# The last feed-forward layer: one more inner block without the seven-product scheme, and products 5 and 2 exchanged in a group's last unit

## The chip, the cores and the metric

The kernel runs on one core of one Trainium2 chip. The time is the device time of one execution in microseconds (us). The kernel before was timed three times: 1418.72 us in the median, 1417.37 to 1418.97 us. Its profile is of a further execution, which took 1418.3 us, and whose span from the first to the last instruction is 1416.1 us.

The engines carry these names in the profile: PE (matrix multiply), PEld (its weight loads), DVE (vector engine), ACT (scalar engine), POOL, and SP, which issues the transfers from memory.

## The reference

Two layers of a transformer-like network act on 128 context tokens and 512 latent tokens of width 1024. Layer 0 has a pooling and convolution mixer, layer 1 has attention; each is followed by a SwiGLU feed-forward network (FFN) with inner width 2816. Everything is in 32-bit floating point. The change lies in the FFN of layer 1, which is the last large piece of work:

```python
D_FF = ((8 * D_MODEL // 3 + 255) // 256) * 256      # 2816

def swiglu(h, w_in, w_out):
    a, b = jnp.split(h @ w_in, 2, axis=-1)
    return (jax.nn.silu(a) * b) @ w_out

        h = modulate(x, norm_g[l, 1], sh2, sc2)
        x = x + g2 * swiglu(h, w_ffn_in[l], w_ffn_out[l])
    y_sample = rms_norm(x, final_g)
```

`modulate` is an RMS norm with a scale and a shift, one pair for the context tokens and one for the latent tokens. The final RMS norm is all that follows this FFN.

## The kernel before

**Layout.** Activations are held transposed: the features lie on the 128 partitions, in eight blocks `k`, and all 640 tokens lie along the free dimension, in two halves of 320. Both token groups go through together. Each 32-bit operand is split into a high and a low part (`wh`, `wl` for weights, `ah`/`al`, `bh`/`bl`, `xh`/`xl` for activations); a matrix product is the sum of three matmuls: high by high, high by low, low by high. The split of a tile is always the same pair of instructions, the high part by ACT (L142) and then the low part by DVE (L143).

**The FFN in groups.** The 22 inner blocks of 128 go in three groups, 0 to 7, 8 to 15 and 16 to 21. A group first computes its inner blocks (`fi`, input projection, SiLU and product; in names `fi1_0_5` is layer 1, group 0, projection 5), keeps them as `ah`/`al` (`keep`), and then adds its part of the output projection to `x` (`fo`).

**Plain blocks.** In layer 1 the inner blocks 0 to `PLAIN - 1` are computed plainly: two projections for each block (the `a` half, then the `b` half), each of eight `k` by three matmuls by two token halves, 48 matmuls of 128x320. They work on the scaled but not yet normalised `x` and multiply by `rstd` afterwards (L503), so they can start before the norm is there. Their results are evacuated by DVE and ACT (`ea`, `eb`).

**Seven products.** All other inner blocks of layer 1 (`fast_blocks`) are units of seven products, in place of the eight block products of a 2x2 by 2x2 multiplication: the 1024 input features are halved, the tokens are halved, and the block's `a` and `b` halves are the two column blocks. A product is four `k` by three matmuls of 128x320, so a unit is 84 matmuls where a plain block is 96. In exchange DVE has to form sums of weights (`weight`, L228 to L239, on the raw weights in place) and, once, sums of the normalised activations (`operand_in`, which calls `Ops.make`): for each of four `kk`, two normalised tiles `n`, a tile `tt` of differences, and seven operands of 320 tokens, split into `bh`/`bl` and `xh`/`xl`. This operand work is put behind the plain projections 1 to 4 (`in_done`), amid their own evacuations.

The products accumulate in three PSUM banks: products 1 and 2 in `x1` (bank 0), products 6, 5 and 3 in `y` (bank 1), products 7 and 4 in `w` (bank 2); odd and even units use different halves of each bank. After product 1, ACT copies `x1` to `y` (L620), so 6 must wait for that copy. After 6, ACT copies `y` out (L623), so the next product on `y` must wait for it. After 2, ACT takes the SiLU of `x1` (L626). After 5, ACT copies `y` out (L629) and DVE adds `w` to it (L630), so 3 must wait for the copy. After 3, ACT takes the SiLU of `y` (L632). After 4, DVE adds `w` and multiplies by the SiLU (L635, L636), and the block is kept. `fast_order` gives the order of the products: while unit n does 1, 7, 6, 2, 5, the products 3 and 4 of unit n - 1 are put between them. Behind the last unit there is nothing more to put between its products 5, 3 and 4.

**What sets the order.** Outside the start of the kernel the instructions of each engine are put in order by the scheduler of the tile framework when the program is built; each engine then works through its own queue strictly in that order. Split weights live in tiles of two products each with three buffers (`wh`, `wl`), named by the first of the two (`wh_fi1_3_p1` holds products 1 and 7 of block 3). Raw weights have three buffers, 1 MB each, loaded by SP (L218). PSUM tiles of the plain projections and of `fo` take the three banks in turn (`ps_tile`), so the number of projections ahead decides which bank comes next.

## Time and profile before

| what | value |
| --- | --- |
| median of 3 runs | 1418.72 us (1417.37 to 1418.97) |
| profiled execution | 1418.3 us, of it 1416.1 us span |
| busy in the span | PE 1363.3 us (96%), DVE 1011.2 us (71%), ACT 580.2 us (41%), POOL 148.4 us (10%) |
| granted PE clock, mean of the span | 0.980 |
| FFN of layer 1, first matmul of `fi` | 947.5 us |
| first matmul of a seven-product unit | 992.6 us |
| last matmul of a seven-product unit | 1358.3 us |

PE is busy almost throughout, so what the program costs is the number of matmuls, the time that each takes, and the few places where PE stands still or runs at a lower clock. A row of the timeline gives start, duration, engine, line, operation, tiles and, in brackets, how long the engine stood idle before it and which instruction ended that. A row of the windows gives, for a stretch, busy time and number of instructions of each engine (an instruction that reaches over an edge counts in both stretches), then the granted PE clock (1.00 is full speed), the busy share of the transfer engines and GB/s. Matmuls overlap: one of 0.31 us is followed by the next 0.147 to 0.149 us later.

### The profile page before, as it was taken

How to read it: one execution, taken by the hardware profiler on the slowest of the kernel's cores; microseconds unless marked ns; L12 is line 12 of the kernel's file. 1: busy time of each engine (PE TensorE's matmuls, PEld its weight loads, DVE VectorE, ACT ScalarE, POOL GpSimd, SP SyncE). 2: the span in 40 equal slices, each digit the busy share in tenths (PEclk: the TensorE clock that was granted, in tenths of full speed). 3: DMA queues.
4: the chain of work that ended last, by engine and by line, in shares of the span. 5: the costliest groups of instructions: out<-in, count | busy, mean ns of one | idle time of the engine just before them, and what ended most of it. 6: DMA issues, size and time to landing. Idle time of an engine off the chain costs nothing.

```text
span 1416.1 us, 22537 instructions
## 1 busy us (share of the span) xinstructions
PE 1363.3 (96%) x9127; PEld 1332.6 (94%) x9127; DVE 1011.2 (71%) x1963; ACT 580.2 (41%) x1031; POOL 148.4 (10%) x116
## 2 busy tenths in 40 slices
PE   6989998999999999999999999999899999999995
PEld 3889998999999999999999999999899999999995
DVE  4899999777768787754667677688863477536745
ACT  3433334332123221222565676557552255314543
POOL 3451112000000000000303121030000000000003
PEclk7999999999999999999999999999899999999998
DMA  9624544444444444221322111011132022311212
GB/s 364 253 95 161 189 141 161 138 151 147 146 152 145 154 137 161 79 86 59 113 73 92 46 46 38 31 60 60 38 112 90 31 90 89 120 60 60 75 46 75
DMA packets 36728, 154.50 MB, mean 109 GB/s; under 512 B 3984, under 2 KB 11152, under 8 KB 26000
## 3 DMA queue, kind: packets, MB, share of 16 engines
q1 hardware_dynamic: 36624, 153.07, 31.0%
q8 instruction: 71, 1.16, 0.3%
q14 instruction: 33, 0.27, 0.1%
HBM read 147.55 MB, written 2.88 MB: 106 GB/s over the span
## 4 chain that ended last, share of the span: by engine, by line
PE 75%; DVE 18%; issue 2%; ACT 2%; DMA 1%; POOL 1%; SPq 0%; DVEq 0%; POOLq 0%; ACTq 0%
PE fi L285 22%; PE fo L285 21%; PE fi L608 17%; DVE junk L363 6%; PE pq L285 5%; PE wa L285 2%; DVE al L467 2%; PE o L1287 2%; PE s L1237 1%; DVE bl L143 1%; DVE wl_in L143 1%; PE t L1270 1%; DVE x L488 1%; DVE wl_out L143 1%; DMA raw_ada<-wada 1%
## 5 line engine op out<-in xcount | busy, mean ns | idle before, releaser
L363 DVE CUSTOM_DVE_ANT_0 junk<-rawa,silb 128x512 f32<-128x512 f32 x336 | 250.6, 746 | 7.6 <-ACT silb L791 1.0
L285 PE MATMUL fi<-al,wh_fi 128*128 128x320 f32 (+1 forms) x800 | 184.6, 312 | 2.2 <-DVE al L467 2.2
L285 PE MATMUL fi<-ah,wh_fi 128*128 128x320 f32 (+1 forms) x800 | 185.0, 313 | 1.4 <-ACT ah L465 1.4
L285 PE MATMUL fi<-ah,wl_fi 128*128 128x320 f32 (+1 forms) x800 | 184.3, 312 | 0.0
L488 DVE SCALAR_TENSOR_TENSOR x<-fo,mod,x 128x128 f32<-128x128 f32 (+1 forms) x144 | 54.6, 434 | 135.0 <-PE fo L285 131.7
L285 PEld LDWEIGHTS fi<-al,wh_fi 128*128 128x128 f32 x800 | 136.0, 190 | 2.7 <-DVE al L467 2.7
L285 PEld LDWEIGHTS fi<-ah,wh_fi 128*128 128x128 f32 x800 | 136.3, 191 | 1.6 <-ACT ah L465 1.6
L285 PEld LDWEIGHTS fi<-ah,wl_fi 128*128 128x128 f32 x800 | 135.8, 190 | 0.0
L143 DVE TENSOR_TENSOR wl_fi_p<-raw_fi,wh_fi_p 128x512 fp32r<-128x512 f32 x133 | 90.1, 688 | 53.9 <-ACT wh_fi_p L142 53.9
L142 ACT ACTIVATE wh_fi_p<-raw_fi 128x512 fp32r<-128x512 f32 x133 | 81.0, 627 | 110.8 <-PE fi L608 66.0
L142 ACT ACTIVATE wh_fi<-raw_fi 128x1024 fp32r<-128x1024 f32 x50 | 52.9, 1059 | 171.8 <-PE fi L285 134.6
L142 ACT ACTIVATE wh_fo<-raw_fo 128x1024 fp32r<-128x1024 f32 (+1 forms) x48 | 47.5, 990 | 178.9 <-PE fo L285 131.2
L608 PE MATMUL fi<-bh,wh_fi_p 128*128 128x320 f32 x304 | 94.7, 311 | 4.1 <-ACT bh L142 2.2
L608 PE MATMUL fi<-bl,wh_fi_p 128*128 128x320 f32 x304 | 94.2, 310 | 0.5 <-DVE bl L143 0.5
L608 PE MATMUL fi<-bh,wl_fi_p 128*128 128x320 f32 x304 | 94.5, 311 | 0.0
L285 PE MATMUL fo<-bh,wh_fo 128*128 128x320 f32 x352 | 80.6, 310 | 0.0
L285 PE MATMUL fo<-bh,wl_fo 128*128 128x320 f32 x352 | 80.5, 310 | 0.0
L285 PE MATMUL fo<-bl,wh_fo 128*128 128x320 f32 x352 | 80.4, 310 | 0.0
L422 POOL TENSOR_TENSOR ssq_b<-ssq_b,sq_b 128x640 f32<-128x640 f32 x14 | 25.2, 1803 | 516.1 <-ACT sq_b L420 516.1
L285 PE MATMUL fo<-al,wh_fo 128*128 128x320 f32 x328 | 75.0, 310 | 0.0
L285 PE MATMUL fo<-ah,wl_fo 128*128 128x320 f32 x328 | 74.9, 309 | 0.0
L285 PE MATMUL fo<-ah,wh_fo 128*128 128x320 f32 x328 | 74.8, 309 | 0.0
(342 smaller groups left out, 3348.5 us busy)
## 6 DMA issues: line engine op xcount, KB each, us to landing
raw_fi<-wfi SPq DMA_DIRECT2D x44, 1024.0 KB, 4.8
rawa<-wada SPq DMA_DIRECT2D x84, 512.0 KB, 3.5
raw_fo<-wfo SPq DMA_DIRECT2D x16, 1024.0 KB, 4.9
raw_ada<-wada SPq DMA_DIRECT2D x12, 512.0 KB, 9.3
raw_in<-win SPq DMA_DIRECT2D x6, 1024.0 KB, 6.5
raw_fo<-wfo SPq DMA_DIRECT2D x8, 768.0 KB, 4.2
raw_qkv<-wqkv SPq DMA_DIRECT2D x6, 1024.0 KB, 4.8
raw_out<-wout SPq DMA_DIRECT2D x4, 1024.0 KB, 4.9
```

The lines of the kernel that those rows point to most:

```text
L142: S.activation(h, src, AF.Copy)
L143: eng.tensor_tensor(out=l, in0=src, in1=h.bitcast(F32), op=ALU.subtract)
L285: PE.matmul(ps[:, h, 0 : hi - lo], w[a][:, k, cols], rhs[b][:, k0 + k, lo:hi], start=k == 0 and a == b, stop=k == kn - 1 and a == 1,)
L363: op = V.tensor_tensor_reduce(out=junk, in0=raw[:, cols], in1=silb[:, c, cols], scale=1.0, scalar=0.0, op0=ALU.mult, op1=ALU.add, accum_ou ...
L422: (eng or G).tensor_tensor(out=self.acc[:, cols], in0=self.acc[:, cols], in1=sq[:, cols], op=ALU.add)
L467: V.scalar_tensor_tensor(out=lo[:, k, a:b], in0=x[:, k, a:b], scalar=s[:, k, c : c + 1], in1=h[:, k, a:b].bitcast(F32), op0=ALU.mult, op1= ...
L488: V.scalar_tensor_tensor(out=xs, in0=got[:, 0 : b - a], scalar=mod[l][:, gate0 + m, c : c + 1], in1=xs, op0=ALU.mult, op1=ALU.add,)
L608: PE.matmul(out, w[a][:, k, :], ops.get(OPERAND[p], b)[:, k, :], start=fresh and k == 0 and a == b, stop=k == ops.kn - 1 and a == 1, skip_ ...
L1237: PE.matmul(self.ps[:, hf, 0:HT], bufB[a][:, self.h, q0 : q0 + P], kt[b][:, self.kv, hf * HT : hf * HT + HT], start=n == 0, stop=n == 2,)
L1270: PE.transpose(flat(pt)[:, s * P : s * P + P], self.pe[:, s * P : s * P + P], ident)
L1287: PE.matmul(po[:, 0 : 2 * P], vt[a][:, self.kv, s * P : s * P + P], got[b][:, s, :], start=s == 0 and n == 0, stop=s == 4 and n == 2,)
```

## The change

`PLAIN` goes from 3 to 4. Group 0 of the last FFN then computes the blocks 0 to 3 plainly, with eight projections where there were six, and the blocks 4 to 7 in seven products, four units where there were five. Layer 0, which has no seven-product units, stays as it is. The operand work stays behind the projections 1 to 4.

In `fast_order` the last unit of each group (there are three) gets product 5 ahead of product 2. With n the last unit, the order at its end was 1, 7, 3 of n - 1, 6, 4 of n - 1, 2, 5, then 3, 4; it becomes 1, 7, 3 of n - 1, 6, 4 of n - 1, 5, 2, then 3, 4.

```diff
@@ -31,7 +31,7 @@
 GROUPS = ((0, 8), (8, 16), (16, 22))
 
 FAST = (1,)
-PLAIN = 3
+PLAIN = 4
 RAW = 3
 WINDOWS = (2, 4, 8, 16)
 PAD = 8
@@ -178,6 +178,8 @@
         out = []
         for n in range(units + 1):
             seq = ((n, 1), (n, 7), (n - 1, 3), (n, 6), (n - 1, 4), (n, 2), (n, 5))
+            if n == units - 1:
+                seq = seq[:5] + ((n, 5), (n, 2))
             out += [(u, p) for u, p in seq if 0 <= u < units]
         return out
 
```

How this moves the instructions in the built program is shown at three places. Line numbers of the changed kernel are two higher from L181 on; the numbers at the ends of names are buffer numbers.

DVE in group 0, where the operands for `kk` = 3 are formed (`n_7`, `n_3`, `tt`; low parts `bl`, `xl`). Before:

```order
L677 TENSOR_TENSOR n_7_9635<-x_67,rstd_83 128x640
L143 TENSOR_TENSOR wl_fi1_3_p1_9575<-raw_fi1_3_9249,wh_fi1_3_p1_9574 128x512
L143 TENSOR_TENSOR wl_fi1_3_p6_9658<-raw_fi1_3_9249,wh_fi1_3_p6_9657 128x512
L234 TENSOR_TENSOR raw_fi1_3_9249<-raw_fi1_3_9249 128x4x128
L584 TENSOR_TENSOR tt_9639<-n_7_9635,n_3_9631 128x320
L143 TENSOR_TENSOR bl_71<-n_7_9635,bh_70 128x2x320
L585 TENSOR_TENSOR n_3_9631<-n_3_9631 128x320
L143 TENSOR_TENSOR wl_fi1_3_p6_9658<-raw_fi1_3_9249,wh_fi1_3_p6_9657 128x512
L586 TENSOR_TENSOR tt_9639<-n_7_9635,n_3_9631 128x320
L143 TENSOR_TENSOR bl_71<-n_3_9631,bh_70 128x2x320
L589 TENSOR_TENSOR n_7_9635<-n_7_9635,tt_9639 128x320
L143 TENSOR_TENSOR xl_9243<-tt_9639,xh_9242 128x2x320
```

With the change:

```order
L679 TENSOR_TENSOR n_7_9631<-x_67,rstd_83 128x640
L143 TENSOR_TENSOR wl_fi1_3_1_9708<-raw_fi1_3_9249,wh_fi1_3_1_9707 128x1024
L143 TENSOR_TENSOR wl_fi1_4_p1_9714<-raw_fi1_4_9412,wh_fi1_4_p1_9713 128x512
L586 TENSOR_TENSOR tt_9635<-n_7_9631,n_3_9627 128x320
L143 TENSOR_TENSOR bl_71<-n_7_9631,bh_70 128x2x320
L587 TENSOR_TENSOR n_3_9627<-n_3_9627 128x320
L505 TENSOR_TENSOR eb1_2_9701<-fi1_0_5_9648,rstd_83 128x640
L588 TENSOR_TENSOR tt_9635<-n_7_9631,n_3_9627 128x320
L143 TENSOR_TENSOR bl_71<-n_3_9627,bh_70 128x2x320
L591 TENSOR_TENSOR n_7_9631<-n_7_9631,tt_9635 128x320
L143 TENSOR_TENSOR xl_9243<-tt_9635,xh_9242 128x2x320
L143 TENSOR_TENSOR xl_9243<-n_7_9631,xh_9242 128x320
```

The operand rows keep their order. Where four weight rows for products of block 3 stood among them, there are now the second half of block 3's plain weights, the first product of block 4, and the evacuation of projection 5.

PE in group 0, from product 1 to product 6 of the first unit (bank 0 is `fi1_0_0`, bank 1 `fi1_0_1`, bank 2 `fi1_0_2`). Before, the last three matmuls of products 1 and 7, the start of `y` (L602) and then product 6:

```order
L608 MATMUL fi1_0_0_9714<-bh_70,wh_fi1_3_p1_9574 128x320
L608 MATMUL fi1_0_0_9714<-bl_71,wh_fi1_3_p1_9574 128x320
L608 MATMUL fi1_0_0_9714<-bh_70,wl_fi1_3_p1_9575 128x320
L608 MATMUL fi1_0_2_9716<-xh_9242,wh_fi1_3_p1_9574 128x320
L608 MATMUL fi1_0_2_9716<-xl_9243,wh_fi1_3_p1_9574 128x320
L608 MATMUL fi1_0_2_9716<-xh_9242,wl_fi1_3_p1_9575 128x320
L602 MATMUL fi1_0_1_9715<-bh_70,onesr_75 128x320 x2
L608 MATMUL fi1_0_1_9715<-xh_9242,wh_fi1_3_p6_9657 128x320
L608 MATMUL fi1_0_1_9715<-xl_9243,wh_fi1_3_p6_9657 128x320
L608 MATMUL fi1_0_1_9715<-xh_9242,wl_fi1_3_p6_9658 128x320
```

With the change, the same place in block 4:

```order
L610 MATMUL fi1_0_0_9832<-bh_70,wh_fi1_4_p1_9713 128x320
L610 MATMUL fi1_0_0_9832<-bl_71,wh_fi1_4_p1_9713 128x320
L610 MATMUL fi1_0_0_9832<-bh_70,wl_fi1_4_p1_9714 128x320
L610 MATMUL fi1_0_2_9834<-xl_9243,wh_fi1_4_p1_9713 128x320
L610 MATMUL fi1_0_2_9834<-xh_9242,wl_fi1_4_p1_9714 128x320
L610 MATMUL fi1_0_1_9833<-xh_9242,wh_fi1_4_p6_9775 128x320
L610 MATMUL fi1_0_1_9833<-xl_9243,wh_fi1_4_p6_9775 128x320
L610 MATMUL fi1_0_1_9833<-xh_9242,wl_fi1_4_p6_9776 128x320
```

The start of `y` and ten matmuls of product 7 now stand ahead of product 1, and two matmuls of product 7 behind it.

ACT at the end of group 1, from the copy after product 6 of block 15 (`uv` is L623 and L629, `sa` is L626 and L632 before). Before:

```order
L142 ACTIVATE wh_fi1_15_p3_11705<-raw_fi1_15_11410 128x512
L623 ACTIVATE uv_11690<-fi1_1_1_10798 128x320
L142 ACTIVATE wh_fo1_1_0_0_11770<-raw_fo1_1_0_11534 128x1024
L142 ACTIVATE ah_68<-uv_11568 128x640
L626 ACTIVATE sa_11729<-fi1_1_0_10797 128x320
L142 ACTIVATE wh_fo1_1_0_1_11779<-raw_fo1_1_0_11534 128x1024
L629 ACTIVATE uv_11690<-fi1_1_1_10798 128x320
L632 ACTIVATE sa_11729<-fi1_1_1_10798 128x320
```

With the change:

```order
L142 ACTIVATE wh_fi1_15_p3_11701<-raw_fi1_15_11406 128x512
L625 ACTIVATE uv_11686<-fi1_1_1_10794 128x320
L142 ACTIVATE wh_fo1_1_0_0_11766<-raw_fo1_1_0_11530 128x1024
L142 ACTIVATE ah_68<-uv_11564 128x640
L631 ACTIVATE uv_11686<-fi1_1_1_10794 128x320
L142 ACTIVATE wh_fo1_1_0_1_11775<-raw_fo1_1_0_11530 128x1024
L628 ACTIVATE sa_11739<-fi1_1_0_10793 128x320
L634 ACTIVATE sa_11739<-fi1_1_1_10794 128x320
```

The copy after product 5 (L629 before, L631 now) has moved ahead of the split of the second half of `fo`'s first weights.

## The prediction

> **What bounds the kernel now.** I began with the first two parts of the page, to see which engine fills the span.

> ```profile
> span 1416.1 us, 22537 instructions
> ...
> PE 1363.3 (96%) x9127; PEld 1332.6 (94%) x9127; DVE 1011.2 (71%) x1963; ACT 580.2 (41%) x1031; POOL 148.4 (10%) x116
> ...
> PEclk7999999999999999999999999999899999999998
> ```

> PE is busy for 96% of the span. In the row of its clock, each digit stands for a fortieth of the span (35.4 us); the 29th, from 991 to 1027 us, is an 8 amid nines. The changed code runs there. So I asked next for PE's waits from 880 us to the end:

> ```profile
> PE ms_fin L446 <- DVE ssq_fin L422: 2.2, 1, 2.2
> PE fi L608 <- ACT bh L142: 2.2, 1, 2.2
> PE fi L608 <- ACT uv L629: 1.9, 2, 1.4
> PE fi L285 <- DVE al L467: 1.4, 1, 1.4
> ...
> PE fi L608 <- ACT fi L620: 0.6, 1, 0.6
> PE fi L608 <- DVE bl L143: 0.5, 1, 0.5
> PE fi L602 <- ACT eb L508: 0.4, 1, 0.4
> ```

> The columns are total, times, longest. Two places matter. The rows on `bh`, `bl`, `fi` L620 and `eb` are one stretch, where the seven products begin: 3.7 us together. The row on `uv` L629 is the copy after product 5, late at two group ends: 1.9 us. The waits on `ssq_fin` and `al` lie outside the change.

> The waits understate the first place. PE's timeline and the windows:

> ```profile
> 992.61 0.31 PE L608 MATMUL fi<-bh,wh_fi_p 128*128 128x320 f32 x1
> ...
> 995.10 0.31 PE L608 MATMUL fi<-xh,wl_fi_p 128*128 128x320 f32 x1
> 997.61 0.41 PE L608 MATMUL fi<-bh,wh_fi_p 128*128 128x320 f32 x1 [2.20 <-ACT bh L142]
> 998.51 0.63 PE L608 MATMUL fi<-bl,wh_fi_p 128*128 128x320 f32 x1 [0.48 <-DVE bl L143]
> ```

> ```profile
> 956.79:992.53 35.74, 35.74 (x243) 35.74 (x242) 31.42 (x52) 27.12 (x52) 0.00 (x0) 1.00 0.17 60
> 965.02:999.99 34.97, 32.28 (x210) 31.42 (x209) 33.93 (x58) 27.53 (x50) 0.00 (x0) 0.97 0.09 31
> 992.60:1008.50 15.90, 12.21 (x51) 10.54 (x50) 14.26 (x25) 7.58 (x14) 0.00 (x0) 0.68 0.00 1
> 1146.00:1171.30 25.30, 25.28 (x169) 24.56 (x169) 19.14 (x31) 13.29 (x27) 0.00 (x0) 1.00 0.25 84
> 994.80:998.20 3.40, 1.02 (x6) 0.53 (x4) 3.40 (x7) 3.21 (x6) 0.00 (x0) 1.00 0.00 0
> 998.20:1008.40 10.20, 8.88 (x29) 7.71 (x30) 8.66 (x15) 2.53 (x6) 0.00 (x0) 0.50 0.00 1
> ```

> From 992.60 to 1008.50 PE started about 50 matmuls. At the rate of two undisturbed units (168 matmuls in 25.30 us, 0.151 us each) these take 7.5 us; they took 15.9. This place loses 8.4 us, less than half of it by standing still. The rest is the clock: from 998.20 to 1008.40 it was granted at 0.50, after 3.4 us in which PE was busy for only 1.02.

> Why are the operands late? DVE was busy for 33.93 of the 34.97 us from 965.02 to 999.99 (its number is the third of the windows). It is the engine behind; the chain of waits says the same:

> ```profile
> 993.37 1.20 DVE wl_fi_p L143 x2
> 994.57 0.60 DVE raw_fi L234
> ...
> 998.85 1.14 DVE xl L143 x2
> 999.99 0.74 DVE eb L503
> ...
> 1000.76 0.18 ACT eb L508
> ```

> DVE forms the last operand (`xl`) at 999.99, when PE has been short of operands since 995.2, and weight conversions for products stand amid the operands.

> **The change part by part.** *Block 3 plain.* The plain stretch from 956.79 to 992.53 holds 240 matmuls in 35.74 us, so 96 take 14.3 us. A unit takes 12.65 us (half of 25.30). So +1.6 us, on PE and so on the path.

> *The start of the seven products.* They now begin 14.3 us later, about 1006.9. I walk DVE's queue from where it first differs, with its timeline:

> ```profile
> 975.25 1.21 DVE L143 TENSOR_TENSOR wl_fi<-raw_fi,wh_fi 128x1024 fp32r<-128x1024 f32 x1
> ...
> 984.81 0.68 DVE L143 TENSOR_TENSOR wl_fi_p<-raw_fi,wh_fi_p 128x512 fp32r<-128x512 f32 x1
> 985.53 0.69 DVE L232 TENSOR_TENSOR raw_fi<-raw_fi 128x512 f32<-128x512 f32 x1
> 986.25 0.69 DVE L236 TENSOR_TENSOR raw_fi<-raw_fi 128x512 f32<-128x512 f32 x1
> 986.86 0.48 DVE L584 TENSOR_TENSOR tt<-n,n 128x320 f32<-128x320 f32 x1
> ```

> Three rows (984.81 to 986.86, 2.05 us) give way to one half of plain weights (1.2 us): 0.85 us sooner. Amid `kk` = 3, four weight rows of 0.6 (2.4) give way to 1.2 for the second half, 0.6 for the first product of block 4, and 0.74 for evacuating projection 5, which stood behind the operands (2.5). So the last operand comes near 999.2, 7.7 us before PE wants it. Up to product 7's weights DVE then has seven instructions (the rest of block 2, the evacuation of projection 6, a weight sum, two splits, one `keep`), at the mean of the stretch (33.93 / 58 = 0.585) 4.1 us: they are there at 1003.3, 3.6 us ahead. The plain block's own weights are split by about 986 and 993.8, and PE wants them at 992.6 and 999.7. DVE's surplus of work is absorbed by block 3, and with the wait goes the clock's reason. This removes 8.4 us.

> Something new appears. Bank 0 is now projection 7's, the last one; product 1 waits for its evacuation (DVE 0.74, ACT 0.18). Ahead of it stand L602 and ten matmuls of product 7, 12 steps of 0.147 (1125.31 to 1125.45 and on, below) or 1.8 us, which cover that. But between product 1 and product 6 only two matmuls of 7 are left to cover the copy L620. Group 1 shows that hand-over with four:

> ```profile
> 1125.31 0.31 PE L608 MATMUL fi<-bh,wl_fi_p 128*128 128x320 f32 x1
> 1125.45 0.31 PE L608 MATMUL fi<-xh,wl_fi_p 128*128 128x320 f32 x1
> ...
> 1125.88 0.31 PE L608 MATMUL fi<-xh,wl_fi_p 128*128 128x320 f32 x1
> 1126.13 0.42 PE L608 MATMUL fi<-xh,wh_fi_p 128*128 128x320 f32 x1
> ```

> From product 1's last matmul (1125.31) to product 6's first (1126.13) are 0.82 us; with two between, PE would need 0.44, so it waits 0.4 us. ACT's queue has a `keep` ahead of that copy, so I take +0.5, with 0 (all covered) and 1.5 (evacuation, 0.9, and a hand-over of 0.6 bare) as bounds.

> *Product 5 ahead of 2.* At the end of group 1 ACT did this, and PE below it:

> ```profile
> 1219.86 1.06 ACT L142 ACTIVATE wh_fo<-raw_fo 128x1024 fp32r<-128x1024 f32 x1 [0.95 <-PE fi L608]
> 1220.82 0.42 ACT L629 ACTIVATE uv<-fi 128x320 f32<-128x320 f32 x1
> ```

> ```profile
> 1219.60 0.31 PE L608 MATMUL fi<-bh,wl_fi_p 128*128 128x320 f32 x1
> 1221.29 0.42 PE L608 MATMUL fi<-bh,wh_fi_p 128*128 128x320 f32 x1 [1.39 <-ACT uv L629]
> ```

> ACT's queue held a `wh_fo` split that waited for PE to release a weight buffer, and the copy stood behind it; PE's product 3 waited 1.39 us, and 0.5 us at the end of group 0. Now the copy stands ahead of that split, and the twelve matmuls of product 2 (1.8 us) cover it. That is -1.9 us. Group 2 has no such wait in PE's list; nothing is gained.

> In turn product 5 now follows 6 on the same bank with only five matmuls of product 4 between. By the 0.82 us above, six steps of 0.147 (0.88) just cover the copy L623, if ACT is free:

> ```profile
> 1215.72 0.44 ACT L623 ACTIVATE uv<-fi 128x320 f32<-128x320 f32 x1 [1.59 <-PE fi L608]
> ```

> It had stood idle for 1.59 us, so it is. I take +0.1 for each of three ends; the bounds are 0 and 0.5, as the end of group 0 shows for a late copy. DVE and ACT lose one unit's weight sums and splits, off the path. SP's loads keep their order.

> The sum: +1.6 - 8.4 + 0.5 - 1.9 + 0.3 = -7.9 us. Idle time leaves out what a matmul takes longer behind a wait: from start to start (1219.60 to 1221.29, less one step) group 1's end costs 1.54, not 1.39. With 0.15 more at both ends the sum is -8.2 us. Against the profiled execution, 1418.3 us (2.2 us outside the span), that is 1410.1; the median of the runs is 0.4 higher. I forecast **1410.2 us**. The bounds are -9.3 (no new wait, and the first place reckoned at the bare step of 0.147 and group 1's hand-over covered too, 0.3 together) and -6.0 (1.5 and three times 0.5). With half a microsecond for the spread of the runs the likeliest case reaches from 1408.6 to 1413.0.

> **The rivals.** *The half clock stays.* It may have its own period rather than follow the wait. For it: waits of 1.4 us (1221.29, and `al` above) had no such stretch after them, so the threshold is not seen; against it: PE was busy for under a third of the 3.4 us ahead, and an earlier half-clock stretch also lies where PE was mostly idle:

> ```profile
> 86.90:93.60 6.70, 3.58 (x13) 3.58 (x14) 6.70 (x20) 3.55 (x6) 0.33 (x4) 0.50 0.25 79
> ```

> In 10.2 us at half clock half the work is done, so 5.1 us are lost: 1415.3 us. [...]

> *The operands stay late.* If DVE slips by the 7.7 us of slack, for instance as it waits in its strict queue for PE to free a weight buffer (`wl_fi1_4_p1` among the operands needs projection 5 done, 992.6, and stands at about 993.5), the first place keeps its 8.4 us: 1418.3 + 1.6 - 1.9 + 0.3 = 1418.3, no change. The margin of 0.9 us in front of that one row is thin, but missing it costs only what it is missed by.

> *Slower: the copy after product 6 is blocked.* ACT's queue is strict, and `wh_fi1_15_p3` stands ahead of L623. If it waits for a buffer as `wh_fo` did, PE stands still between 6 and 5 at all three ends. With 1.4 us each (4.2) the change still gains; it turns slower once two of the stops grow to the size of the first place, with its half clock: 2 x 8.4 = 16.8, so 1427 us. The point is about 4 us a stop. The buffer in question is released by product 3 of the unit before, well ahead of 6.

> **How the numbers follow.** The forecast 0.84, half clock stays 0.07, operands late 0.06, copy blocked 0.03. A measurement of this kernel can tell about 0.2% (2.8 us) from no change. Faster by more than that: the first two, 0.91; within: 0.06; slower: 0.03. The range, 1408.2 to 1414.0 us, is the likeliest one's own, with 0.4 below for terms that I left at zero and 1.0 above for a half-clock stretch that is only shortened; it leaves out the rivals at 1415.3, 1418.3 and 1427, together 0.16.

> **What would show it.** Right: no wait on `bh` or `bl` at L610 (L608 before); first seven-product matmul at about 1007, no clock below 1.00 in the 30 us behind it; no wait on L631 (L629 before); 12 more matmuls. A wait of about half a microsecond at L610 on L622 (L620 before). Wrong: a half-clock stretch after 1007; operand splits on DVE later than 1003; a wait on L625 (L623 before) above half a microsecond; or a wait of the plain matmuls on `wl_fi`.

## The result and the profile after

The changed kernel takes 1409.70 us in the median (1408.83 to 1410.30, four runs); the kernel before, run beside it, takes 1418.37 us (1417.37 to 1418.97, four runs). The ratio is 0.9939 (0.9922 to 0.9956): 8.7 us faster, and the time forecast was 1410.2 us. The profiled execution of the changed kernel took 1408.83 us, of it 1406.9 us span.

The head of its page, with the row of the granted clock:

```profile
span 1406.9 us, 22549 instructions
...
PE 1361.5 (97%) x9139; PEld 1332.9 (95%) x9139; DVE 1006.5 (72%) x1955; ACT 578.1 (41%) x1025; POOL 148.4 (11%) x116
...
PEclk7999999999999999999999999999999999999998
```

There are 12 more matmuls and PE is busy for 1.8 us less: the 8 in the row of the clock, where a part of the work ran at half clock, is gone. All of PE's waits from 880 us to the end:

```profile
PE ms_fin L448 <- DVE ssq_fin L424: 2.2, 1, 2.2
PE fi L287 <- DVE al L469: 1.5, 1, 1.5
PE t L1272 <- DVE pt_0l L143: 0.6, 1, 0.6
PE fi L610 <- ACT fi L622: 0.2, 1, 0.2
```

Of the waits in the region of the change one is left, of 0.2 us; `bh`, `bl` and the copy after product 5 (L631 now) no longer appear. The windows of the plain stretch, of the first unit's start, and of the 30 us around and behind it:

```profile
957.00:1007.58 50.58, 50.58 (x343) 50.58 (x342) 45.51 (x75) 36.95 (x67) 0.00 (x0) 1.00 0.18 63
1007.58:1023.00 15.42, 15.20 (x105) 14.94 (x104) 11.55 (x19) 7.89 (x17) 0.00 (x0) 1.00 0.19 68
1004.00:1034.00 30.00, 29.76 (x200) 29.09 (x200) 24.11 (x39) 16.21 (x33) 0.00 (x0) 1.00 0.17 55
```

In the 15.4 us from the start of the seven products PE now starts 105 matmuls at a clock of 1.00, where before it started about 50 in 15.9 us at 0.68. The operands are why. DVE's timeline shows the last operand (`xl`) and the low part of product 7's weights, PE's timeline the start of `y` (L604), which precedes the first product:

```profile
999.22 0.81 DVE L143 TENSOR_TENSOR xl<-tt,xh 128x640 fp32r<-128x640 f32 x1
999.96 0.48 DVE L143 TENSOR_TENSOR xl<-n,xh 128x320 fp32r<-128x320 f32 x1
...
1003.96 0.68 DVE L143 TENSOR_TENSOR wl_fi_p<-raw_fi,wh_fi_p 128x512 fp32r<-128x512 f32 x1
```

```profile
1007.58 0.46 PE L604 MATMUL fi<-bh,onesr 128*128 128x320 f32 x2
...
1011.22 0.30 PE L610 MATMUL fi<-xh,wl_fi_p 128*128 128x320 f32 x1
1011.75 0.42 PE L610 MATMUL fi<-xh,wh_fi_p 128*128 128x320 f32 x1 [0.22 <-ACT fi L622]
```

The operands are complete at 1000.4 us, 7.1 us before PE begins the products. The one new stop lies at 1011.75: 0.53 us from start to start, 0.38 us more than a step of 0.147.

At the end of group 1, ACT and PE:

```profile
1208.11 0.44 ACT L625 ACTIVATE uv<-fi 128x320 f32<-128x320 f32 x1 [1.59 <-PE fi L610]
1208.70 1.07 ACT L142 ACTIVATE wh_fo<-raw_fo 128x1024 fp32r<-128x1024 f32 x1
...
1210.88 0.42 ACT L631 ACTIVATE uv<-fi 128x320 f32<-128x320 f32 x1
1212.31 1.06 ACT L142 ACTIVATE wh_fo<-raw_fo 128x1024 fp32r<-128x1024 f32 x1 [1.01 <-PE fi L610]
```

```profile
1212.06 0.31 PE L610 MATMUL fi<-bh,wl_fi_p 128*128 128x320 f32 x1
1212.20 0.31 PE L610 MATMUL fi<-bh,wh_fi_p 128*128 128x320 f32 x1
```

The copy L631 ends at 1211.30, 0.9 us before product 3 starts at 1212.20 without a stop. The `wh_fo` split behind the copy still waits 1.01 us, for the same reason as before, but nothing that PE needs stands behind it.

Where the time went, by stages of the two traces (each from the start of its first PE row; the first `fi` matmul is at 947.51 us before and at 948.14 us now, 0.6 us that lie ahead of the change):

| stage | before, us | after, us | difference, us |
| --- | --- | --- | --- |
| plain blocks and products of group 0 | 117.84 | 110.21 | -7.62 |
| `fo` of group 0 | 56.80 | 56.54 | -0.26 |
| products of group 1 | 102.77 | 100.81 | -1.96 |
| `fo` of group 1 | 56.54 | 56.54 | 0.00 |
| group 2 to the end | 134.70 | 134.70 | 0.00 |
| first `fi` to the end | 468.64 | 458.80 | -9.84 |

The 0.26 us at `fo` of group 0 are two steps at its start, of 0.29 and 0.25 us at 1066 us, that run at the bare rate now.

### The profile page after: what moved, and what is told of

The parts are those of the page before. It is cut to its first block, busy times and chain, and to the rows that moved or that the text cites. A ratio compares the mean times of both kernels' runs of the same rounds, so it can differ in the third digit from the quotient of the medians.

```text
span 1406.9 us, 22549 instructions
## 1 busy us (share of the span) xinstructions
PE 1361.5 (97%) x9139; PEld 1332.9 (95%) x9139; DVE 1006.5 (72%) x1955; ACT 578.1 (41%) x1025; POOL 148.4 (11%) x116
## 4 chain that ended last, share of the span: by engine, by line
PE 78%; DVE 16%; issue 2%; ACT 2%; DMA 1%; POOL 1%; SPq 0%; DVEq 0%; POOLq 0%; ACTq 0%
PE fi L287 26%; PE fo L287 21%; PE fi L610 16%; DVE junk L365 6%; PE pq L287 5%; PE wa L287 2%; DVE al L469 2%; PE o L1289 2%; PE s L1239 1%; DVE wl_in L143 1%; PE t L1272 1%; DVE x L490 1%; DVE wl_out L143 1%; DVE bl L143 1%; DMA raw_ada<-wada 1%
## 5 line engine op out<-in xcount | busy, mean ns | idle before, releaser
L287 PE MATMUL fi<-al,wh_fi 128*128 128x320 f32 x832 | 192.2, 312 | 2.2 <-DVE al L469 2.2
L287 PE MATMUL fi<-ah,wh_fi 128*128 128x320 f32 x832 | 192.5, 313 | 1.4 <-ACT ah L467 1.4
L287 PE MATMUL fi<-ah,wl_fi 128*128 128x320 f32 x832 | 191.6, 312 | 0.0
L287 PEld LDWEIGHTS fi<-al,wh_fi 128*128 128x128 f32 x832 | 141.7, 190 | 2.8 <-DVE al L469 2.8
L287 PEld LDWEIGHTS fi<-ah,wh_fi 128*128 128x128 f32 x832 | 141.7, 191 | 1.6 <-ACT ah L467 1.6
L287 PEld LDWEIGHTS fi<-ah,wl_fi 128*128 128x128 f32 x832 | 141.4, 190 | 0.0
L142 ACT ACTIVATE wh_fi<-raw_fi 128x1024 fp32r<-128x1024 f32 x52 | 55.0, 1058 | 172.0 <-PE fi L287 134.8
L142 ACT ACTIVATE wh_fi_p<-raw_fi 128x512 fp32r<-128x512 f32 x126 | 77.3, 627 | 111.8 <-PE fi L610 65.0
L142 ACT ACTIVATE wh_fo<-raw_fo 128x1024 fp32r<-128x1024 f32 (+1 forms) x48 | 47.5, 991 | 180.5 <-PE fo L287 132.6
L143 DVE TENSOR_TENSOR wl_fi_p<-raw_fi,wh_fi_p 128x512 fp32r<-128x512 f32 x126 | 85.6, 688 | 48.5 <-ACT wh_fi_p L142 48.2
L610 PE MATMUL fi<-bh,wl_fi_p 128*128 128x320 f32 x288 | 88.9, 309 | 0.0
L610 PE MATMUL fi<-bh,wh_fi_p 128*128 128x320 f32 x288 | 88.7, 308 | 0.0
L610 PE MATMUL fi<-bl,wh_fi_p 128*128 128x320 f32 x288 | 88.3, 307 | 0.0
```

Of the source, the lines that this page charges most:

```text
L142: S.activation(h, src, AF.Copy)
L143: eng.tensor_tensor(out=l, in0=src, in1=h.bitcast(F32), op=ALU.subtract)
L287: PE.matmul(ps[:, h, 0 : hi - lo], w[a][:, k, cols], rhs[b][:, k0 + k, lo:hi], start=k == 0 and a == b, stop=k == kn - 1 and a == 1,)
L610: PE.matmul(out, w[a][:, k, :], ops.get(OPERAND[p], b)[:, k, :], start=fresh and k == 0 and a == b, stop=k == ops.kn - 1 and a == 1, skip_ ...
```

## Experiments

The theory was that two separate stalls went: the operands' lateness at the start of the products, with the half clock that it brings, and the place of the copy in ACT's queue at the group ends. The rivals were that the half clock has a cause of its own, that the block of plain work as such is what pays, and that one part does all the work.

**One part at a time.** The kernel before with the plain block alone:

```diff
-PLAIN = 3
+PLAIN = 4
```

> The kernel before with four plain blocks, order of products as before. If the two parts of the change act apart: the wait and the half clock at the first product are gone, the waits on the copy after product 5 stay. Before the change they cost 1.5 and 0.7 us counted from start to start, so 2.2 us above the changed kernel's 1409.7: 1411.9 us, with a wait of about 1.4 us on that copy at the end of group 1. Rival (the exchange alone earns nothing, since the longer plain stretch shifts the queues and so the copy is in time anyway): 1409.7 us and no such wait.

Measured: 1411.81 us (1411.46 to 1412.92), ratio to before 0.9955 (0.9942 to 0.9969). And the changed kernel without it, so that only the exchange of products 5 and 2 is left:

```diff
-PLAIN = 4
+PLAIN = 3
```

> The kernel before with product 5 ahead of 2 in each group's last unit, three plain blocks. If the parts act apart: the start of the products keeps its waits and its half-clock stretch of 10 us, the two group ends lose theirs: 1418.4 - 2.2 = 1416.2 us. Rival (the wait on product 5's copy turns into one on product 6's copy): no change, 1418.4 us, with waits on that copy of 0.5 us or more.

Measured: 1416.16 us (1415.18 to 1418.46), ratio 0.9986 (0.9977 to 0.9995). From the first `fi` matmul to the end the two take 7.02 and 2.79 us less than before; together 9.8, as the whole change does (9.84). The parts add up, since they lie at different places. PE's waits, first with the plain block alone, then with the exchange alone, and a window of the latter:

```profile
PE fi L608 <- ACT uv L629: 1.4, 1, 1.4
PE fo L285 <- ACT wh_fo L142: 0.8, 1, 0.8
...
PE fi L608 <- ACT fi L620: 0.2, 1, 0.2
```

```profile
PE fi L610 <- ACT bh L142: 2.2, 1, 2.2
```

```profile
998.10:1008.34 10.24, 8.75 (x29) 7.51 (x29) 8.90 (x15) 2.77 (x6) 0.00 (x0) 0.50 0.00 1
```

With the plain block alone the start is clean and the copy after product 5 is late; with the exchange alone it is the reverse, half clock included. One thing was not foreseen: with the plain block alone it is the end of group 0 that loses 1.4 us (0.5 before). At the end of group 1, ten matmuls of `fo` now stand ahead of product 3 and cover the copy; at the end of group 2, three do, and PE waits 0.8 us for the `wh_fo` split that they read. ACT's and PE's timelines at the end of group 0:

```profile
1055.32 1.06 ACT L142 ACTIVATE wh_fo<-raw_fo 128x1024 fp32r<-128x1024 f32 x1 [0.97 <-PE fi L608]
1056.29 0.42 ACT L629 ACTIVATE uv<-fi 128x320 f32<-128x320 f32 x1
```

```profile
1055.06 0.31 PE L608 MATMUL fi<-bh,wl_fi_p 128*128 128x320 f32 x1
1056.76 0.41 PE L608 MATMUL fi<-bh,wh_fi_p 128*128 128x320 f32 x1 [1.38 <-ACT uv L629]
```

It is the pair of rows that the prediction showed of group 1: a `wh_fo` split waits 0.97 us for PE, and the copy stands behind it. So the shift of one block moves this trap from one group to another; the exchange takes it away. The 0.5 us of the kernel before at the end of group 0 was not this trap: there the split ended at 1061.15, before product 5 did, and product 3 waited for the bare copy.

**One more plain block.** If plain work as such paid, five blocks would pay again; if the start is already clean, the fifth costs the price of a block.

```diff
-PLAIN = 4
+PLAIN = 5
```

> The changed kernel with five plain blocks. If a plain block in place of a unit costs what its matmuls cost, and the first plain block has already removed the whole wait: 14.3 - 12.6 = 1.6 us more, 1411.3 us. Rival (DVE is still behind after four blocks, and more distance goes on paying): not above 1409.7 us.

Measured: 1410.16 us (1409.32 to 1410.97), ratio to before 0.9943 (0.9930 to 0.9955). The medians, 0.5 us apart, can't be told from each other. The traces can: the plain blocks and products of group 0 take 111.52 us against 110.21, +1.31 us, although the new stop of 0.38 us is gone with the bank order. So a plain block costs about 1.7 us, and the fifth gains nothing.

**The operands late again.** The changed kernel, with the operand work put behind the plain projections 3 to 6 in place of 1 to 4. The number of plain blocks and the exchange stay.

```diff
-                if l in FAST and 1 <= i <= 4:
-                    operand_in(i - 1)
+                if l in FAST and 3 <= i <= 6:
+                    operand_in(i - 3)
```

> The changed kernel with the operand work two projections later (behind projections 3 to 6 in place of 1 to 4), as near to the first product as it was before the change; the number of matmuls is that of the changed kernel. If the operands' lateness is the cause, and the half clock follows from the wait: both are back, up to 8.4 us, 1416 to 1418 us. Rival 1 (the half clock has its own period): the wait is back but the clock stays at 1.00, 2 to 4 us, 1412 to 1414 us. Rival 2 (block 3 itself, its weights or banks, and not the operands, had been in the way): 1409.7 us.

Measured: 1417.36 us (1416.06 to 1418.50), ratio 0.9993 (0.9984 to 1.0002): the gain at the start is gone. PE's wait, and the windows ahead of the fall of the clock and behind it:

```profile
PE fi L610 <- ACT xh L142: 3.9, 1, 3.9
```

```profile
1009.74:1013.15 3.41, 0.00 (x0) 0.00 (x0) 3.41 (x7) 2.64 (x5) 0.00 (x0) 1.00 0.01 2
1013.16:1019.99 6.83, 5.11 (x15) 3.96 (x15) 6.83 (x13) 2.74 (x6) 0.00 (x0) 0.50 0.00 0
```

The order of operand work alone brings the wait back, now in block 4, and the half clock comes with it, 15 us later in the program than before. It has no place of its own.

**A smaller dose.** The same, with the first three pieces one projection late and the last one two:

```diff
-                if l in FAST and 1 <= i <= 4:
-                    operand_in(i - 1)
+                if l in FAST and i in (2, 3, 4, 6):
+                    operand_in((2, 3, 4, 6).index(i))
```

> The changed kernel with the operand work behind the projections 2, 3, 4 and 6, so that only the last quarter of it is late. In the changed kernel that quarter ends at 1000.4; two projections later (14.3 us) and with less between it should end near 1012, when product 7 wants it at about 1009.2: a wait of 1.5 to 3 us, between the change (none) and operands two projections late (3.9 us). If the wait pulls the clock down only from about 2 us on (waits of 1.4 to 1.75 us elsewhere in these traces did not, 2.2 us did): 1411 to 1412 us with a wait under 2 us and clock 1.00, or 1414 to 1417 us with a wait above it and a half-clock stretch. Rival (any wait at this place brings the half clock, since its window is fixed in time): half clock even with a wait under 1.5 us.

Measured: 1413.02 us (1412.13 to 1415.62), ratio 0.9961 (0.9946 to 0.9977). The profiled execution has a wait and the half clock after it:

```profile
PE fi L610 <- ACT eb L510: 2.2, 1, 2.2
```

```profile
1007.75:1011.16 3.41, 1.71 (x10) 1.19 (x9) 3.41 (x6) 2.29 (x5) 0.00 (x0) 1.00 0.00 0
1011.17:1021.41 10.24, 8.92 (x32) 8.52 (x33) 8.20 (x14) 2.98 (x7) 0.00 (x0) 0.50 0.00 0
```

A wait of 2.2 us, 1.4 us of it in this window, and one of 0.3 us ahead of it left PE busy for 1.71 of 3.41 us, and 10.2 us at a clock of 0.50 followed. The four runs spread over 3.5 us, where those of the changed kernel spread over 1.5. The mean granted clock of each whole run fits a half-clock stretch that comes and goes: it is 0.981 in the two longer runs and 0.984 in the two shorter ones, and a stretch of 10.24 us takes 0.0036 off it. But with five blocks it varies as well, from 0.983 to 0.986, so this is not shown.

**Operands early without the plain block.** If lateness is the cause, three plain blocks with operands that come sooner should gain the same and save the block's 1.7 us. First by moving work to POOL, which is idle there (`xl` for the first three `kk`, the product of `ea` and `eb`, and the `keep` of the plain blocks):

```diff
-PLAIN = 4
+PLAIN = 3
...
+            low = G if kk < 3 else V
-            pair(self.dst(4, kk, 2), halves(t[:, 0:T]))
-            pair(self.dst(6, kk), b2[:, H1])
+            pair(self.dst(4, kk, 2), halves(t[:, 0:T]), eng=low)
+            pair(self.dst(6, kk), b2[:, H1], eng=low)
...
+            if l in FAST:
+                for c, a, b in SEG:
+                    G.tensor_scalar(eb[:, a:b], eb[:, a:b], bias(eb, c), None, op0=ALU.add)
+                G.tensor_tensor(out=ea[:, 0:T], in0=eb[:, 0:T], in1=ea[:, 0:T], op=ALU.mult)
+                return
...
-                    keep(j, held.pop(j))
+                    keep(j, held.pop(j), G)
```

> The changed kernel with three plain blocks again, and DVE relieved otherwise: the low parts of the operands xl for kk 0 to 2, the bias and product of the plain blocks and the low parts of their kept results go to POOL, some 5 to 7 us of DVE's queue ahead of the first product. If DVE's lateness is the whole cause and POOL does not slow DVE: no wait above 1 us at the first product, clock 1.00, and the plain block's price is saved: 1408.2 us (1407.5 to 1409.5). Rival 1 (POOL's own spans, 1.8 us for 128x640, make the operands late in DVE's place): wait of 2 us or more on an operand of POOL, 1413 us or more. Rival 2 (POOL slows DVE's instructions while it runs): DVE's 128x640 splits longer than 0.82 us.

Measured: 1422.01 us (1421.30 to 1422.91), ratio 1.0027 (1.0017 to 1.0038), slower than before; 1408.2 was expected. PE's wait for the operands grew:

```profile
PE fi L611 <- ACT bh L142: 6.7, 1, 6.7
```

The groups of DVE's instructions from 965 to 1000 us, of the kernel before and then of this one (busy time, mean ns of one), and the timelines of DVE and POOL in this one:

```profile
L677 DVE TENSOR_TENSOR n<-x,rstd 128x640 f32<-128x640 f32 x8 | 6.3, 816 | 0.0
```

```profile
L685 DVE TENSOR_TENSOR n<-x,rstd 128x640 f32<-128x640 f32 x8 | 10.8, 1394 | 0.0
```

```profile
989.31 1.85 DVE L587 TENSOR_TENSOR n<-n 128x320 f32<-128x320 f32 x1
...
993.36 0.81 DVE L505 TENSOR_TENSOR ea<-fi,rstd 128x640 f32<-128x640 f32 x1
994.09 3.52 DVE L685 TENSOR_TENSOR n<-x,rstd 128x640 f32<-128x640 f32 x2
```

```profile
988.80 2.01 POOL L668 TENSOR_TENSOR ea<-eb,ea 128x640 f32<-128x640 f32 x1
993.16 1.68 POOL L143 TENSOR_TENSOR xl<-tt,xh 128x640 fp32r<-128x640 f32 x1 [2.35 <-ACT xh L142]
994.80 2.13 POOL L143 TENSOR_TENSOR al<-ea,ah 128x640 fp32r<-128x640 f32 x1
996.89 1.44 POOL L143 TENSOR_TENSOR xl<-n,xh 128x320 fp32r<-128x320 f32 x1
```

DVE's work was not relieved: beside POOL's its instructions took longer. The `n` at 989.31 takes 1.85 us where it takes 0.48 elsewhere, and ends 0.35 us after POOL's product, which ends at 990.81; two `n` at 994.09 take 3.52 us while POOL forms `xl` and `al`. `ea` at 993.36, one of whose inputs is in PSUM, takes its usual 0.81 us with POOL at work. What holds the one up and not the other was not shown.

Then by order alone: the operand work one projection earlier, behind 0 to 3, with three plain blocks.

```diff
-PLAIN = 4
+PLAIN = 3
...
-                if l in FAST and 1 <= i <= 4:
-                    operand_in(i - 1)
+                if l in FAST and i <= 3:
+                    operand_in(i)
```

> Three plain blocks, product 5 ahead of 2, and the operand work one projection earlier (behind projections 0 to 3). DVE stood idle for 1.95 us before it began, so the last operand should come at about 998.0 in place of 999.99. In all traces so far, on a fixed grid of 3.41 us, the clock fell to half after a window in which PE was busy for 1.85 us or less, and not after one with 1.92 us or more. If that is the rule: the stop at the first product shrinks from 3.7 us to about 2, so PE is busy for 1.4 to 2 us of the window, on the edge; with the half clock 1413 to 1415 us, without it 1409.5 to 1411 us. Rival (the half clock does not depend on PE's idle time): a half-clock stretch of 10 us whatever the wait.

Measured: 1414.53 us (1414.10 to 1415.00), ratio 0.9969 (0.9958 to 0.9980). The waits are smaller (1.5, 0.9, 0.8 and 0.6 us), but close together, and the half clock stays. Three windows in a row:

```profile
994.29:997.70 3.41, 1.86 (x12) 1.54 (x11) 3.41 (x7) 3.41 (x8) 0.00 (x0) 1.00 0.00 0
997.70:1001.12 3.42, 1.74 (x7) 1.00 (x7) 3.42 (x7) 0.95 (x3) 0.00 (x0) 1.00 0.00 0
1001.12:1007.95 6.83, 6.26 (x24) 6.11 (x24) 6.06 (x11) 2.12 (x4) 0.00 (x0) 0.50 0.00 1
```

And with DVE's product of `ea` and `eb` put off as well, to the plain blocks' `keep` (two more buffers for it):

```diff
-    tpool = ctx.enter_context(tc.tile_pool(name="tpool", bufs=8))
+    tpool = ctx.enter_context(tc.tile_pool(name="tpool", bufs=10))
...
+        late = {}
...
+            if l in FAST:
+                late[j] = eb
+            else:
+                gate(ea, eb)
...
+                    gate(held[j], late.pop(j))
                     keep(j, held.pop(j))
```

> As the kernel with the operand work one projection earlier, and the product of a plain block's two halves (two DVE instructions, 0.93 us for each block) moved from behind its second projection to where the block is kept, after the first product (with ten in place of eight temporary tiles, so that the halves can wait). That takes another 1.9 us from DVE ahead of the first product: last operand at about 996.2, 1 us after PE wants it. By the rule of the window (busy for over 1.92 of 3.41 us) there is no half clock: the price of the plain block is saved (1.3 to 1.6 us) and up to 1 us of waits paid: 1408.3 to 1409.8 us, at or below the changed kernel's 1409.7. Rival (the work put behind the first product delays the product weights there): waits of 1 us or more at L610 within 15 us of the first product, 1411 us or more.

Measured: 1413.12 us (1411.69 to 1415.24), ratio 0.9963 (0.9950 to 0.9977); 1408.3 to 1409.8 was expected. The profiled execution has no half clock, but the waits remain:

```profile
PE fi L610 <- ACT fi L622: 1.1, 2, 0.6
PE fi L610 <- DVE xl L143: 0.9, 1, 0.9
...
```

```profile
967.86 0.49 DVE L586 TENSOR_TENSOR tt<-n,n 128x320 f32<-128x320 f32 x1 [3.28 <-ACT n L689]
...
998.17 0.48 DVE L143 TENSOR_TENSOR xl<-n,xh 128x320 fp32r<-128x320 f32 x1
```

The last `xl` was expected at 996.2 and came at 998.17: DVE stood idle for 3.28 us at the start of the operand work, waiting for ACT's part of the norm, which the earlier place in DVE's queue does not hasten. Two of the five runs took over 1414.5 us, and what they lost this trace does not show. None of these versions reaches the changed kernel; the block of 1.7 us buys slack that the reordering did not.

**Queue or cover at the group ends?** The exchange does two things: it puts the copy ahead of the `wh_fo` split, and it gives it the twelve matmuls of product 2 as cover. To part them, the kernel before with the plain block and that one copy on DVE, products in the old order:

```diff
-PLAIN = 3
+PLAIN = 4
...
-                S.activation(t, y, AF.Copy)
+                if n == len(js) - 1:
+                    V.tensor_copy(t, y)
+                else:
+                    S.activation(t, y, AF.Copy)
```

> Four plain blocks and the order of products as before, with the copy after product 5 in each group's last unit made by DVE in place of ACT, where it stands ahead of the second fo split. It takes away ACT's queue but leaves product 3 right behind product 5. With product 5's copy behind the split on ACT the ends wait 1.4 us (1411.8 us in all); with product 2 between they wait 0 (1409.7 us). If the queue is the larger half: waits of 0.4 to 0.7 us on that copy at each end, 1410.4 to 1411.2 us. Rival (only the cover counts; the copy alone takes as long): waits of 1.2 us or more, 1411.8 us.

Measured: 1412.40 us (1410.61 to 1412.58), ratio 0.9956 (0.9944 to 0.9969), above the 1410.4 to 1411.2 us expected and not to be told from the plain block alone (1411.81). The time is inconclusive; the trace says more:

```profile
PE fi L608 <- DVE uv L630: 1.2, 2, 0.6
```

Out of ACT's queue the copy still costs PE 0.6 us at the ends of groups 0 and 2, in place of 1.4 us on the copy and 0.8 us on the split. At the end of group 0 the queue makes up about 0.8 of the 1.4 us; the bare copy, with no product between, is the other 0.6, close to the 0.5 us of the kernel before there. Only the exchange removes both.

## Why the prediction was right

**Block 3 plain, +1.6 us.** Right: about 1.7 by the fifth block.

**The start of the products, -8.4 us.** Right in its mechanism. Forecast were the last operand complete at 999.2, product 7's weights at 1003.3, the first product at 1006.9 and a clock of 1.00 behind it; measured were 1000.4, 1004.6, 1007.6 and 1.00. The whole program stood 0.6 us later in this execution, and operands and weights came another 0.6 to 0.7 us later than walked, so the slack of 7.7 us came out at 7.1. One step of the walk was off, the "0.85 us sooner": the three rows did give way to one of 1.2 us, but then DVE stood idle for 0.49 us, until ACT's part of `n` was there:

```profile
987.20 0.49 DVE L586 TENSOR_TENSOR tt<-n,n 128x320 f32<-128x320 f32 x1 [0.49 <-ACT n L681]
```

It cost nothing, since the slack was more than ten times as long. The size of the gain was 0.5 us short: the steps from start to start in the first unit of before exceed the bare 0.146 us by 8.9 us in sum, those of the first unit now by 0.5. The net is -8.4, where the prediction's two terms give -7.9, since they reckoned the undisturbed rate at the mean of whole units, 0.151; the prediction had that as its lower bound.

**The copy of product 1, +0.5 us.** It is there, at the place named, with 0.38 us in the step (526 ns less 147) and 0.11 in the one behind it.

**The group ends, -2.2 us.** Right: the two stops from start to start, 1.55 and 0.69 us, are gone. The exchange alone gives 2.8 us from the first `fi` to the end, 0.5 to 0.6 more than the two stops. The step behind each stop, 0.25 us in place of 0.147, goes with it, another 0.2 us. At the end of group 2, where the prediction saw nothing to gain, two steps of 0.31 and 0.25 us at the copy (1354.80 and 1355.05) run at the bare rate, 0.27 us.

**The copy between products 6 and 5, +0.3 us.** This term was too high. Five matmuls all but cover the copy: PE has no wait there, and of the steps one is longer at each end, 0.21 us behind the first matmul of product 5 (1051.51, 1208.86 and 1341.04), so 0.2 us in all.

**The rivals.** That the half clock stays is refuted by the changed kernel, and by the late operands, which brought it back at another time. This rival reckoned with half the work at half clock; in the trace before a step took 0.267 us there (from 1003.15 to 1008.22 us), 1.8 times the 0.147 at full clock, so the 10.24 us lost about 4.6, not 5.1. That the operands stay late did not happen, but the late-operand run gives its price: 1417.36 us where the rival had 1418.3. The copy after 6 was not blocked. The row from 86.90 to 93.60 us, which the prediction read as PE mostly idle, shows it busy for 3.58 of 6.70 us, inside the half-clock stretch; the row that bears on the argument is the window ahead of that stretch (83.46 to 86.87 us, PE busy for 0.78 of 3.41), and it agrees.

Set against the stage table the sum of -8.2 us was 1.6 us short of the traces' -9.84: 0.5 at the start, 0.1 for the copy after 6, 0.2 for the steps behind the two stops, 0.3 at the end of group 2, 0.2 for the hand-over of product 1 in group 1 (the step at 1126.13, which the prediction had in its bound, and the one behind it run at the bare rate now) and 0.26 at the start of `fo` of group 0, where nothing was forecast. The forecast time came within 0.5 us of the median, which is closer than the sum deserved: the profiled execution of the changed kernel is 0.9 us faster than its median, and the forecast takes its 8.2 us from about 1418.4 us, not from the 1418.7 us of the median. The medians differ by 8.7 us; the interval of the ratio (6.2 to 11.1 us) does not part the two sums.

## What to carry to other kernels

Where an engine that is nearly always busy stands still for a moment, compare its steps from start to start, and look at the granted clock of the 10 us that follow: here waits of 3.7 us cost 8.9. A slower form of work can pay when it lets the engine behind catch up: 1.7 us of extra matmuls bought 7 us of slack, and a second dose bought nothing. In a strict queue, look at what stands ahead of a short instruction on the critical path, and move its producer rather than the engine that executes it: the other engine took only a part of the wait away, and with POOL as a helper DVE's `n` went from 816 to 1394 ns.

## What the runs showed of the hardware

**The clock behind a stop.** In the traces of the kernel before and of the changed one the half-clock stretches last 3.41, 6.83, 10.24, 17.07 and 20.48 us, but for the last one of each, which the end of the program cuts off. The table gives PE's busy time in the 3.41 us just ahead of a fall of the clock. Where the clock did not fall, the window was placed by counting in steps of 3.413 us from another stretch; that placing is the author's estimate. More rows, of the run with POOL, of the plain block alone and, early in the program, of the exchange alone and of the kernel before; the others stand above:

```profile
1006.14:1009.55 3.41, 1.85 (x10) 1.32 (x10) 2.79 (x6) 1.47 (x4) 1.60 (x2) 1.00 0.00 0
```

```profile
1054.17:1057.58 3.41, 2.03 (x14) 1.76 (x13) 2.13 (x4) 1.57 (x3) 0.00 (x0) 1.00 0.10 43
```

```profile
158.42:161.83 3.41, 1.60 (x11) 1.34 (x9) 3.41 (x10) 1.27 (x3) 0.00 (x0) 1.00 0.48 154
```

```profile
8.37:11.78 3.41, 1.67 (x8) 0.09 (x4) 0.00 (x0) 0.60 (x1) 0.00 (x0) 1.00 1.00 419
11.78:15.19 3.41, 1.47 (x9) 0.61 (x9) 0.00 (x0) 0.00 (x0) 2.64 (x3) 1.00 1.02 408
15.19:32.26 17.07, 12.66 (x48) 9.07 (x49) 12.82 (x18) 8.52 (x17) 7.29 (x5) 0.50 1.05 389
```

| window | PE busy, us of 3.41 | clock after it |
| --- | --- | --- |
| operands late | 0.00 | 0.50 |
| before, 994.80 | 1.02 | 0.50 |
| before, 11.78 | 1.47 | 0.50 |
| exchange alone, 158.42 | 1.60 | 1.00 |
| before, 8.37 | 1.67 | 1.00 |
| smaller dose | 1.71 | 0.50 |
| operands early, 997.70 | 1.74 | 0.50 |
| work on POOL, 1006.14 | 1.85 | 0.50 |
| operands early, 994.29 | 1.86 | 1.00 |
| plain block alone, 1054.17 | 2.03 | 1.00 |

**POOL against DVE.** DVE's `n` went from 816 to 1394 ns in the mean with POOL's elementwise work beside it; the long ones at 989.31 and 994.09 end 0.35 and 0.68 us after an instruction of POOL's. The evacuations `ea` and `eb`, with an input in PSUM, kept 810 and 818 ns in the mean, where the kernel before has 814 and 819. Nothing was gained by it in this run: PE's wait for `bh` grew from 2.2 to 6.7 us.
